# Delta rule: the triangular solve's two steps per half-level on ScalarE instead of VectorE, with N masked by GpSimd and the sums formed in PSUM

## The chip, the cores and the metric

The kernel runs on one core of a Trainium2 chip. The metric is the device time of one execution in microseconds; a comparison uses the median of several runs. Engine names are those of the profile: PE is TensorE (matrix products), PEld its weight loads, DVE is VectorE, ACT is ScalarE, POOL is GpSimd and SP is SyncE, which here only issues DMA. Each engine takes its instructions strictly in the order of its own queue and waits at semaphores for the others.

## The reference

One decoder layer over a prompt of 1024 tokens and 64 sample tokens, in fp32: RMSNorm, one input projection, two parallel token mixers (retention, and RWKV-7 time mixing), output projection, a product-key expert mixer (PEER) and a gated input embedding. The change touches the RWKV-7 scan, which for each of 8 heads with 64 channels is a delta rule:

```python
def step(S, xs):
    rt, lwt, kt, kkt, at, vt = xs
    sa = jnp.einsum('bhij,bhj->bhi', S, -kkt)
    S = (S * jnp.exp(lwt)[:, :, None, :] + sa[..., None] * (kkt * at)[:, :, None, :]
         + vt[..., None] * kt[:, :, None, :])
    y = jnp.einsum('bhij,bhj->bhi', S, rt)
    return S, y
```

## The kernel before, in words

Tokens come in nine tiles: 0 to 7 are 128 prompt tokens each, tile 8 holds the 64 sample tokens. The scan is done per tile in its chunked form. With the masked products of the tile's vectors in Q (L801 to L804), the corrections U of a tile solve a triangular system, U = (I - strict part)^-1 X, for all 8 heads.

*The solve* (L821 to L852). Z starts as the inverse within pairs of tokens: a DVE product with a mask (L824) and an addition of the identity on POOL (L825). N is Q transposed (L818, L819). Five levels m = 2, 4, 8, 16, 32 then double the blocks that are inverted; tile 8 has two. The heads are two halves s of four. At each level and half (a "half-level"):

- PE transposes Z (L837), and ACT copies it to Tt (L839);
- PE multiplies N with the odd blocks' columns Zs of Z, 4 products of 64 columns into pG (L842), and DVE copies that to G, times a 0/1 mask for the level (L844);
- PE multiplies Tt and G into pZG (L849), and DVE adds that to Zs in place (L851).

The three PSUM tiles of a half come from tag "b" with three buffers (tiles 0 and 8: "b" and "d").

*After the solve.* DVE scales the state into S0 (L857). pX is the product of the state with the tile's vectors plus Kq times V, in one PSUM tile (L868 to L876); ACT copies it to X (L879). For prompt tiles the last step of the inverse is done by halves of 64 tokens: U of the lower half (L901, L903), its part in the upper half into pL (L895), added to X by DVE (L897), then U of the upper half. The new state (L908, L918, L919) and the output pY (L963, L964) follow.

*What runs beside it.* `group_b` goes over the tiles in the order 1, 8, 2 to 7 and interleaves three or four generators: the solve and the rest of one tile (`cur`), the retention and preparation of the next up to "chain" (`nxt`), the output projection of an earlier tile (`c_rows`: weights cw streamed from memory, products ewo, L610), and `early`. Each `yield` hands over to the next generator. The framework then sets the order on each engine's queue by its own simulated timeline, so the order moves as a whole when instructions change.

`early` is the expert mixer of tiles 0, 1 and 8. A short query phase loads ewq (L1189) and multiplies (epq, L1194). Then, for each of 128 (tile 8: 64) expert slots, POOL issues an indirect DMA that gathers 128 rows of 4 KB (grow, L1126) into one of four slots of a ring, and DVE uses it: with in_pu in L1140 (a dot product with x, which lies in PSUM), with in_pv in L1154 (added to gacc in PSUM).

After the tiles come the queries of the dense part (`c_query`, PE), the top-k of tiles 4 to 7 (DVE, with what is left of `early`), and a dense pass over all experts (py, ph). Tile 0's solve runs earlier, from 150 to 210 us, beside the input projection.

Of the kernel before, what the change touches and what calls it, by code (L numbers as in the profile page):

```python
# [44 lines left out]
def consts():  # L45
# [26 lines left out]
    lev = np.zeros((128, 5, 64), np.float32)  # L72
    for i, m in enumerate(LEVELS):
        for qq in range(64):
            b = qq // m
            lev[b * 2 * m:b * 2 * m + m, i, qq] = 1.0
# [134 lines left out]
class K:  # L211
# [46 lines left out]
    def setup_mix(self, es):  # L258
# [435 lines left out]
    def rw_mix(self, t):  # L694
# [132 lines left out]
        lev = self.c("lev").rearrange("p (l q) -> p l q", l=5)  # L827
        nq = n // 2
        for li, m in enumerate(LEVELS):
            if smp and m >= 8:  # L830
                break
            Zs = Z[:n, :, :n].rearrange("p h (c s m) -> p h c s m", s=2, m=m)[:, :, :, 1, :]
            Tt, G, pz = [None] * 2, [None] * 2, [None] * 2
            for s in range(2):
                p = self.ps("trz", hb[s]).rearrange("p (a b) -> p a b", a=4)
                for j in range(4):
                    nc.tensor.transpose(p[:n, j, :n], Z[:n, 4 * s + j, :n], self.c("ident", n)[:, :n])  # L837
                Tt[s] = wp.tile([128, 4, n], F32, name=f"Tt{s}")
                nc.scalar.activation(Tt[s][:n, :, :n], p[:n, :, :n], AF.Copy)  # L839
                p = self.ps("pG", hb[s])[:, :256].rearrange("p (h q) -> p h q", h=4)  # L840
                for j in range(4):
                    nc.tensor.matmul(p[:n, j, :nq], N[:n, 4 * s + j, :n], Zs[:, 4 * s + j], start=True, stop=True)  # L842
# [700 lines left out]
```

## Time and profile before

| | us |
|---|---|
| median of 3 runs | 3937.49 |
| the runs | 3921.43, 3937.49, 3937.65 |
| the profiled execution | 3941.76 |
| its span, first to last instruction | 3940.0 |
| PE busy | 3367.7 (85%) |
| DVE busy | 2961.7 (75%) |
| POOL busy | 2339.6 (59%) |
| ACT busy | 1225.5 (31%) |
| mean granted clock of TensorE | 0.87 |

The page comes from one execution. In the rows of groups, the columns are line, engine, operation, tiles (out<-in), shape and count, then busy time in us and mean ns of one, then the engine's idle time just before them and what ended it. An fp32 product appears as two records, a transpose as one. A busy PE is not PE at its peak, since matmuls are pipelined and their ends are modelled.

### The profile page before, as it was taken

The page shows a single profiled execution, that of the slowest core. Times are in us where ns is not written, and L with a number is a line of the kernel's source. Part 1 is how long each engine was busy: PE and PEld are TensorE (multiplying, and loading weights), DVE is VectorE, ACT ScalarE, POOL GpSimd, SP SyncE. Part 2 cuts the span into 40 slices and gives each one's busy share as a digit, 9 for nine tenths or more (in the row PEclk, how much of TensorE's full clock was granted, in tenths as well). Part 3 has the DMA queues.
Part 4 walks back from the last instruction along what each step waited for, and adds up shares of the span by engine and source line. Part 5 has one row for each costly group of instructions (what it writes and reads, how often), then busy time and mean ns, then how long its engine had stood idle before and what let it go on. Part 6 is the DMA issues. An engine that isn't in the chain of part 4 may idle for free.

```text
span 3940.0 us, 52682 instructions
## 1 busy us (share of the span) xinstructions
PE 3367.7 (85%) x17749; PEld 2768.7 (70%) x17749; DVE 2961.7 (75%) x5764; ACT 1225.5 (31%) x2247; POOL 2339.6 (59%) x2051
## 2 busy tenths in 40 slices
PE   8798985777869776885899899999699988999978
PEld 7687984645747664763788678888588866677757
DVE  4454488977697689886659999987777777777774
ACT  4232221011111111111232266777422333333322
POOL 5353175544454536554567757886488777777740
PEclk9799995666977567676999999999899999999989
DMA  7267568898868878789998748899899999999962
GB/s 256 72 194 234 168 209 266 277 302 267 295 229 285 299 269 283 265 278 332 331 350 295 245 171 302 306 347 344 324 343 341 334 362 357 358 362 349 339 230 70
DMA packets 473864, 1107.20 MB, mean 281 GB/s; under 512 B 74555, under 2 KB 191545, under 8 KB 467642
## 3 DMA queue, kind: packets, MB, share of 16 engines
q0 software_dynamic: 165888, 604.05, 43.0%
q1 hardware_dynamic: 245694, 393.26, 30.5%
q10 hardware_dynamic: 62012, 106.52, 7.2%
q8 instruction: 141, 2.31, 0.2%
q14 instruction: 129, 1.06, 0.1%
HBM read 997.17 MB, written 106.43 MB: 280 GB/s over the span
## 4 chain that ended last, share of the span: by engine, by line
PE 45%; DVE 22%; DMA 16%; issue 7%; POOL 6%; ACT 2%; SPq 0%; ACTq 0%; POOLq 0%; DVEq 0%
PE py L1294 14%; DVE grow L1140 4%; DVE gacc L1154 3%; PE ph L325 3%; PE ph L326 3%; PE ph L327 3%; POOL grow L1126 3%; DMA ewq<-in_wq 2%; PE epq L1194 2%; DMA grow<-in_pv,eid 2%; DMA grow<-in_pu,eid 2%; POOL vl L300 2%; DMA ft<-fd 1%; DVE oh L1240 1%; PE ewo L610 1%
## 5 line engine op out<-in xcount | busy, mean ns | idle before, releaser
L1126 POOL DMA_INDIRECT grow<-in_pv,eid x576 | 569.8, 989 | 507.3 <-DVE gacc L1154 309.4
L1126 POOL DMA_INDIRECT grow<-in_pu,eid x576 | 568.7, 987 | 435.2 <-DVE grow L1140 287.9
L1154 DVE SCALAR_TENSOR_TENSOR gacc<-grow,ac,gacc 128x1024 f32<-128x1024 f32 x571 | 731.8, 1282 | 89.5 <-DMA grow<-in_pv,eid 84.3
L1140 DVE SCALAR_TENSOR_TENSOR grow<-grow,gacc 128x1024 f32<-128x1024 f32 x576 | 691.1, 1213 | 125.0 <-DMA grow<-in_pu,eid 118.3
L1294 PE MATMUL py<-ah,vh 128*128 128x512 f32 x1024 | 408.1, 399 | 40.3 <-ACT ah L296 27.1
L1294 PE MATMUL py<-ah,vl 128*128 128x512 f32 x1024 | 407.1, 403 | 34.1 <-POOL vl L300 34.0
L325 PE MATMUL ph<-cx,uh 128*128 128x512 f32 x1024 | 406.4, 397 | 7.2 <-ACT geh L1262 7.2
L326 PE MATMUL ph<-cx,uh 128*128 128x512 f32 x1024 | 406.4, 397 | 0.0
L327 PE MATMUL ph<-cx,ul 128*128 128x512 f32 x1024 | 405.5, 396 | 1.0 <-POOL ul L300 1.0
L1294 PE MATMUL py<-al,vh 128*128 128x512 f32 x1024 | 405.3, 396 | 0.0
L300 POOL TENSOR_TENSOR vl<-vraw,vh 128x640 fp32r<-128x640 f32 (+2 forms) x224 | 325.4, 1457 | 53.1 <-ACT vh L296 49.3
L300 POOL TENSOR_TENSOR ul<-uraw,uh 128x1024 fp32r<-128x1024 f32 x128 | 308.6, 2412 | 64.5 <-ACT uh L296 62.3
L296 ACT ACTIVATE vh<-vraw 128x640 fp32r<-128x640 f32 (+2 forms) x224 | 154.9, 692 | 393.8 <-PE py L1294 238.3
L1294 PEld LDWEIGHTS py<-ah,vl 128*128 128x128 f32 x1024 | 194.1, 190 | 98.4 <-POOL vl L300 56.1
L1294 PEld LDWEIGHTS py<-ah,vh 128*128 128x128 f32 x1024 | 194.6, 190 | 96.5 <-ACT vh L296 28.7
L1298 DVE TENSOR_TENSOR yT<-yT,py 128x512 f32<-128x512 f32 x216 | 147.4, 684 | 151.5 <-PE py L1294 151.1
L325 PEld LDWEIGHTS ph<-cx,uh 128*128 128x128 f32 x1024 | 194.7, 190 | 48.4 <-ACT geh L1262 8.8
L1294 PEld LDWEIGHTS py<-al,vh 128*128 128x128 f32 x1024 | 194.0, 189 | 43.7
L327 PEld LDWEIGHTS ph<-cx,ul 128*128 128x128 f32 x1024 | 194.9, 190 | 41.6 <-POOL ul L300 1.9
L326 PEld LDWEIGHTS ph<-cx,uh 128*128 128x128 f32 x1024 | 195.0, 190 | 39.1
L296 ACT ACTIVATE uh<-uraw 128x1024 fp32r<-128x1024 f32 x128 | 135.2, 1056 | 246.1 <-PE ph L326 128.5
L300 POOL TENSOR_TENSOR wl<-wraw,wh 128x1024 fp32r<-128x1024 f32 x45 | 110.5, 2455 | 138.8 <-ACT wh L296 138.7
(400 smaller groups left out, 7833.3 us busy)
## 6 DMA issues: line engine op xcount, KB each, us to landing
uraw<-in_puT SPq DMA_DIRECT2D x128, 512.0 KB, 4.8
vraw<-in_pvd SPq DMA_DIRECT2D x152, 320.0 KB, 6.1
cw<-in_w_out SPq DMA_DIRECT2D x128, 256.0 KB, 5.1
wd<-wst ACTq DMA_DIRECT2D x32, 1024.0 KB, 13.1
wt<-wd SPq DMA_DIRECT2D x64, 512.0 KB, 8.0
wraw<-in_w_ret SPq DMA_DIRECT2D x48, 512.0 KB, 4.7
ewq<-in_wq SPq DMA_DIRECT2D x48, 512.0 KB, 6.7
gd<-geh ACTq DMA_DIRECT2D x96, 256.0 KB, 5.0
```

The costliest lines, as they stand in the source:

```text
L296: nc.scalar.activation(hi, src, AF.Copy)
L300: nc.gpsimd.tensor_tensor(lo, src, hi.bitcast(F32), op=OP.subtract)
L325: mm(out, lh(k), rh(k), start=first and k == 0, stop=False)
L326: mm(out, lh(k), rl(k), start=False, stop=False)
L327: mm(out, ll(k), rh(k), start=False, stop=last and k == nk - 1)
L610: nc.tensor.matmul(p[:n], oT[k // 4][:, k % 4, :n], w, start=k == 0, stop=k == 7)
L1126: nc.gpsimd.indirect_dma_start(out=g, out_offset=None, in_=src, in_offset=bass.IndirectOffsetOnAxis(ap=self.eid[t][:, j:j + 1], axis=0))
L1140: nc.vector.scalar_tensor_tensor(g[:, c], g[:, c], 1.0, x[:, c], op0=OP.mult, op1=OP.mult, accum_out=hv[:, i, j:j + 1])
L1154: nc.vector.scalar_tensor_tensor(y[:, c], g[:, c], ac[:, j:j + 1], y[:, c], op0=OP.mult, op1=OP.add)
L1194: nc.tensor.matmul(p[:, :n], w[:, k], xT[:, k, :n], start=k == 0, stop=k == 7)
L1294: nc.tensor.matmul(p, lh[:, b, :], rh, start=b == 0 and j == 0, stop=b == nb - 1 and j == 2)
L1298: nc.vector.tensor_tensor(yT[:, d, :], yT[:, d, :], p, op=OP.add)
```

## The change

GpSimd masks N ahead of the solve: `mask(i)` writes Nm, the N of half-level i times that level's 0/1 mask, now 128 columns wide per level. Two masks are issued before the first half-level, and the one for i + 2 within half-level i; Nm has three buffers. pG is then the product of Nm with Zs and needs no mask, so ACT copies it to G. The sum Z + pZG is formed in PSUM: a product of the identity with Zs (256 columns) opens the accumulation, the four products of Tt and G add to it, and ACT copies the result back to Zs. No DVE instruction is left in the half-level. In a level, pG and the transpose of each half come first (the product now ahead of the transpose), then both pZG.

For prompt tiles, pX is made in two PSUM tiles, one for each half of the tokens ("d" and "b"), each with its own state and V products; the former pL accumulates on the upper one, and ACT copies each half to X. The scaled state S0 is made ahead of the levels. To make room, N has one buffer instead of two, S0 one instead of two, and sg moves into the six-buffer tag t2. Tile 8 keeps its pX.

```diff
-               ("lev", 64 * 5), ("hind", 32), ("seqtok", 8), ("seqfeat", 512), ("gc", 4), ("gc8", 8)):
+               ("lev", 128 * 5), ("hind", 32), ("seqtok", 8), ("seqfeat", 512), ("gc", 4), ("gc8", 8)):
...
-        self.Sb = [[cp.tile([128, 4, 128], F32, name=f"S{a}{b}") for b in range(2)] for a in range(3)]
+        self.Sb = [[cp.tile([128, 4, 128], F32, name=f"S{a}{b}") for b in range(1 + (a < 2))] for a in range(3)]
...
-        sg = wp.tile([128, 512], F32, name="sg")
+        sg = T2("sg") if n == 128 else wp.tile([128, 512], F32, name="sg", tag="t2", bufs=6)
...
-        N = wp.tile([128, 8, n], F32, name="N", bufs=b2)
+        N = wp.tile([128, 8, n], F32, name="N")
...
-            for s in range(2):
-                p = self.ps("trz", hb[s]).rearrange("p (a b) -> p a b", a=4)
-                for j in range(4):
-                    nc.tensor.transpose(p[:n, j, :n], Z[:n, 4 * s + j, :n], self.c("ident", n)[:, :n])
-                Tt[s] = wp.tile([128, 4, n], F32, name=f"Tt{s}")
-                nc.scalar.activation(Tt[s][:n, :, :n], p[:n, :, :n], AF.Copy)
-                p = self.ps("pG", hb[s])[:, :256].rearrange("p (h q) -> p h q", h=4)
-                for j in range(4):
-                    nc.tensor.matmul(p[:n, j, :nq], N[:n, 4 * s + j, :n], Zs[:, 4 * s + j], start=True, stop=True)
-                G[s] = wp.tile([128, 4, n // 2], F32, name=f"G{s}")
-                nc.vector.tensor_tensor(G[s][:n, :, :nq], p[:n, :, :nq], lev[:n, li, None, :nq].to_broadcast([n, 4, nq]), op=OP.mult)
-                yield
-            for s in range(2):
-                p = self.ps("pZG", hb[s])[:, :256].rearrange("p (h q) -> p h q", h=4)
-                for j in range(4):
-                    nc.tensor.matmul(p[:n, j, :nq], Tt[s][:n, j, :n], G[s][:n, j, :nq], start=True, stop=True)
-                pz = p[:n, :, :nq].rearrange("p h (c m) -> p h c m", m=m)
-                nc.vector.tensor_tensor(Zs[:, 4 * s:4 * s + 4], Zs[:, 4 * s:4 * s + 4], pz, op=OP.add)
-                yield
...
+        def mask(i):
+            if i < len(steps):
+                li, s = steps[i]
+                Nm[i] = wp.tile([128, 4, n], F32, name="Nm", bufs=3)
+                nc.gpsimd.tensor_tensor(Nm[i][:n, :, :n], N[:n, 4 * s:4 * s + 4, :n],
+                                        lev[:n, li, None, :n].to_broadcast([n, 4, n]), op=OP.mult)
+
+        mask(0)
+        mask(1)
+        for i, (li, s) in enumerate(steps):
...
+            for j in range(4):
+                nc.tensor.matmul(p[:n, j, :nq], Nm[i][:n, j, :n], Zs[:, 4 * s + j], start=True, stop=True)
+            G[s] = wp.tile([128, 4, n // 2], F32, name=f"G{s}")
+            nc.scalar.activation(G[s][:n, :, :nq], p[:n, :, :nq], AF.Copy)
+            mask(i + 2)
+            p = self.ps("trz", hb[s]).rearrange("p (a b) -> p a b", a=4)
...
+            for s in range(2):
+                p = self.ps("pZG", hb[s])[:, :256].rearrange("p (h q) -> p h q", h=4)
+                zs = Zs[:, 4 * s:4 * s + 4]
+                pz = p[:n, :, :nq].rearrange("p h (c m) -> p h c m", m=m)
+                nc.tensor.matmul(pz, self.c("ident", n)[:, :n], zs, start=True, stop=False)
+                for j in range(4):
+                    nc.tensor.matmul(p[:n, j, :nq], Tt[s][:n, j, :n], G[s][:n, j, :nq], start=False, stop=j == 3)
+                nc.scalar.activation(zs, pz, AF.Copy)
+                yield
...
+            px = {}
+            for half, tag in ((lo, "d"), (up, "b")):
+                p = px[tag] = self.ps("pX", tag)
+                opens = True
+                for hp in range(4):
+                    if not first:
+                        nc.tensor.matmul(p[half, hp * 128:hp * 128 + 128], art[:, hp, 0, half], S0[:, hp, :], start=opens, stop=False)
+                        opens = False
+                    for s in range(2):
+                        h = 2 * hp + s
+                        hs = slice(h * 64, h * 64 + 64)
+                        nc.tensor.matmul(p[half, hs], Kq[:, hq(h), 0, half], V[:, hs], start=opens, stop=half is lo and h == 7)
+                        opens = False
+                yield
...
-                        nc.tensor.matmul(p[up, hs], Q[lo, hq(h), 0, up], U[lo, hs], start=True, stop=True)
+                        nc.tensor.matmul(p[up, hs], Q[lo, hq(h), 0, up], U[lo, hs], start=False, stop=h == 7)
                     yield
-                    nc.vector.tensor_tensor(X[up], X[up], p[up], op=OP.add)
+                nc.scalar.activation(X[half], p[half], AF.Copy)
```

How the order moves is seen in the last tile's solve. DVE's queue there before (gacc<-grow are the gathered rows being used, G and Z the solve):

```order
L981 TENSOR_TENSOR hnx<-hnx,pgt 128x512
L844 TENSOR_TENSOR G_12617<-pG,cstb 128x256
L1154 SCALAR_TENSOR_TENSOR gacc<-grow,ac,gacc 128x1024
L844 TENSOR_TENSOR G_12631<-pG,cstb 128x256
L1154 SCALAR_TENSOR_TENSOR gacc<-grow,ac,gacc 128x1024
L851 TENSOR_TENSOR Z<-Z,pZG 128x128x2 x2
L1154 SCALAR_TENSOR_TENSOR gacc<-grow,ac,gacc 128x1024
L844 TENSOR_TENSOR G_12671<-pG,cstb 128x256
```

and DVE's queue there after the change, up to the tile's new state (S<-pS):

```order
L1007 TENSOR_TENSOR hnx<-hnx,pgt 128x512
L1180 SCALAR_TENSOR_TENSOR gacc<-grow,ac,gacc 128x1024 x10
L610 TENSOR_TENSOR ch<-ewo,ch 128x512
L1180 SCALAR_TENSOR_TENSOR gacc<-grow,ac,gacc 128x1024 x4
L944 TENSOR_TENSOR S_204<-pS,S_205 64x4x64 x2
```

The solve's 20 instructions are gone from between the gathered rows. POOL's queue in the same solve before (grow<-in_pv are the gathers being issued, Z and hnx the tile's own work):

```order
L825 TENSOR_TENSOR Z<-Z,csta 128x1024
L1126 DMA grow<-in_pv,eid_65 128x1024
L970 TENSOR_TENSOR hnx<-hnx,row_ln_g 128x512
L1126 DMA grow<-in_pv,eid_65 128x1024
L971 TENSOR_TENSOR hnx<-hnx,row_ln_b 128x512
L1126 DMA grow<-in_pv,eid_65 128x1024 x2
L974 TENSOR_TENSOR hnx<-hnx,bv 128x512
L1126 DMA grow<-in_pv,eid_65 128x1024 x24
```

and POOL's queue after the change (Nm are the masks):

```order
L838 TENSOR_TENSOR Nm<-N,cstb 128x512
L1152 DMA grow<-in_pv,eid_65 128x1024
L838 TENSOR_TENSOR Nm<-N,cstb 128x512
L1152 DMA grow<-in_pv,eid_65 128x1024
L1000 TENSOR_TENSOR hnx<-hnx,bv 128x512
L838 TENSOR_TENSOR Nm<-N,cstb 128x512
L1152 DMA grow<-in_pv,eid_65 128x1024
L838 TENSOR_TENSOR Nm<-N,cstb 128x512
L1152 DMA grow<-in_pv,eid_65 128x1024 x2
L838 TENSOR_TENSOR Nm<-N,cstb 128x512
```

A run of 24 gathers has become gathers and masks in turn.

More of the change, by code (lines that the diff above doesn't have):

```diff
@@ L71, in consts @@
     put("rel8", rel8)
[L72 to L76, printed above, removed]
+    same = lambda m: p[:, None] // (2 * m) == p[None] // (2 * m)
+    lev = np.stack([same(m) & (p[:, None] // m % 2 == 1) & (p[None] // m % 2 == 0) for m in LEVELS], 1).astype(np.float32)
     put("lev", lev)
@@ L826, in rw_mix @@
         yield "chain"
[L827 to L833, printed above, removed]
[L834 to L852 removed]
         if not first and not smp:
[L854 removed]
+            S0 = self.Sb[2][0]
             for s in range(2):
@@ L857, in rw_mix @@
                 nc.vector.tensor_tensor(S0[ps_, :, ps_], self.Swkv[ps_, :, ps_], pe[ps_, 0, :, None].to_broadcast([64, 4, 64]), op=OP.mult)
+        lev = self.c("lev").rearrange("p (l q) -> p l q", l=5)
+        nq = n // 2
+        steps = [(li, s) for li, m in enumerate(LEVELS) if not smp or m < 8 for s in range(2)]
+        Nm = {}
+        def mask(i):
[7 more added lines that the diff above has]
+        for i, (li, s) in enumerate(steps):
+            m = LEVELS[li]
+            if s == 0:
+                Zs = Z[:n, :, :n].rearrange("p h (c s m) -> p h c s m", s=2, m=m)[:, :, :, 1, :]
+                Tt, G = [None] * 2, [None] * 2
+            p = self.ps("pG", hb[s])[:, :256].rearrange("p (h q) -> p h q", h=4)
+            for j in range(4):
[5 more added lines that the diff above has]
+            for j in range(4):
+                nc.tensor.transpose(p[:n, j, :n], Z[:n, 4 * s + j, :n], self.c("ident", n)[:, :n])
+            Tt[s] = wp.tile([128, 4, n], F32, name=f"Tt{s}")
+            nc.scalar.activation(Tt[s][:n, :, :n], p[:n, :, :n], AF.Copy)
+            yield
+            if s == 0:
+                continue
+            for s in range(2):
[3 more added lines that the diff above has]
+                nc.tensor.matmul(pz, self.c("ident", n)[:, :n], zs, start=True, stop=False)
+                for j in range(4):
+                    nc.tensor.matmul(p[:n, j, :nq], Tt[s][:n, j, :n], G[s][:n, j, :nq], start=False, stop=j == 3)
+                nc.scalar.activation(zs, pz, AF.Copy)
+                yield
         def state_mm(p, hp, j):
@@ L867, in rw_mix @@
         hq = lambda h: (h % 2) * 4 + h // 2
[L868 to L877 removed]
         X = T3("X")
[L879 removed]
         U = T3("U")
         if smp:
+            p = self.ps("pX", "d")
+            for hp in range(4):
+                sq = state_mm(p, hp, 0)
+                for s in range(2):
+                    h = 2 * hp + s
+                    hs = slice(h * 64, h * 64 + 64)
+                    self.seq_mm(p[:n, hs], *sq, s)
+                    nc.tensor.matmul(p[:n, hs], Kq[:n, hq(h), 0, :n], V[:n, hs], start=False, stop=True)
+            yield
+            nc.scalar.activation(X[:n], p[:n], AF.Copy)
             p = self.ps("pU", "d")
```

23 lines of the change are left out of this document (8 added, 15 removed).

## The prediction

> **What bounds the kernel now.** I read the stages first, then the groups of instructions within the stage that holds the change, then who waits there, then the chain. The page gives the span; the windows give the stages (columns: stretch, its length, busy time of PE, PEld, DVE, ACT and POOL with counts, granted clock, DMA share, GB/s).
>
> ```profile
> span 3940.0 us, 52682 instructions
> ...
> 150.00:200.00 50.00, 49.26 (x351) 44.60 (x351) 21.87 (x46) 13.63 (x22) 7.36 (x8) 0.88 0.09 30
> ...
> 600.00:1000.00 400.00, 291.58 (x1516) 210.29 (x1516) 318.84 (x533) 46.64 (x105) 202.60 (x198) 0.63 0.87 279
> 1000.00:1400.00 400.00, 317.57 (x1669) 261.27 (x1669) 299.24 (x620) 58.16 (x138) 199.88 (x198) 0.69 0.81 276
> 1400.00:1810.00 410.00, 327.37 (x1761) 255.96 (x1760) 351.25 (x684) 64.45 (x125) 220.91 (x220) 0.74 0.82 280
> 1900.00:2000.00 100.00, 99.16 (x610) 88.36 (x609) 64.95 (x103) 28.32 (x50) 57.38 (x51) 1.00 0.92 342
> ...
> 2100.00:2200.00 100.00, 96.14 (x420) 78.29 (x420) 100.00 (x429) 28.02 (x35) 77.11 (x54) 1.00 0.81 277
> ...
> 2400.00:2500.00 100.00, 95.39 (x487) 80.03 (x486) 99.97 (x214) 65.94 (x130) 82.81 (x62) 0.98 0.91 330
> ```
>
> Tile 0's solve lies in 150 to 200 us, where PE is full (49.26 of 50). The other eight solves lie between 600 and 1810 us. There no engine is full: DVE 969 us of 1210, PE 936, POOL 623, ACT 169. Queries follow (PE full), then the top-k stage, where DVE is full. So I ask what paces 600 to 1820 us. The groups in it:
>
> ```profile
> L1154 DVE SCALAR_TENSOR_TENSOR gacc<-grow,ac,gacc 128x1024 f32<-128x1024 f32 x229 | 293.3, 1281 | 50.9 <-DMA grow<-in_pv,eid 49.3
> L1140 DVE SCALAR_TENSOR_TENSOR grow<-grow,gacc 128x1024 f32<-128x1024 f32 x233 | 280.4, 1212 | 61.0 <-DMA grow<-in_pu,eid 59.4
> L1126 POOL DMA_INDIRECT grow<-in_pv,eid x234 | 238.2, 1018 | 301.3 <-DVE gacc L1154 216.4 <-DMA grow<-in_pv,eid 24.5 <-DVE hns L409 11.4
> L1126 POOL DMA_INDIRECT grow<-in_pu,eid x230 | 227.1, 987 | 250.9 <-DVE grow L1140 193.8 <-issue 13.5 <-DVE G L844 7.2
> ...
> L610 PE MATMUL ewo<-cw,coT 128*128 128x512 f32 (+1 forms) x224 | 124.2, 666 | 14.4 <-DMA cw<-in_w_out 10.6 <-issue 2.1 <-DVE S L506 0.7
> ...
> L842 PE MATMUL pG<-Z,N 128*128 128x64 f32 (+1 forms) x592 | 93.5, 313 | 0.0
> ...
> L844 DVE TENSOR_TENSOR G<-pG,cstb 128x256 f32<-128x256 f32 (+1 forms) x74 | 30.3, 410 | 31.4 <-PE pG L842 31.1
> L851 DVE TENSOR_TENSOR Z<-Z,pZG 128x256 f32<-128x256 f32 (+1 forms) x74 | 29.6, 405 | 11.2 <-PE pZG L849 10.6
> ...
> L825 POOL TENSOR_TENSOR Z<-Z,csta 128x1024 f32<-128x1024 f32 (+1 forms) x8 | 17.8, 2220 | 1.0 <-DVE Z L824 0.9
> ```
>
> The gathers are a ring: POOL issues a row gather into one of four slots, it lands, DVE uses it, and only then may POOL refill the slot. 234 + 230 gathers in 1220 us are one per 2.63 us, 10.5 us per turn of a slot. The issue rows (last number: us to landing) and the waits (total us, times, longest) show what the turn is made of.
>
> ```profile
> grow<-in_pv,eid POOLq DMA_INDIRECT x234, 6.4
> grow<-in_pu,eid POOLq DMA_INDIRECT x230, 5.8
> ```
> ```profile
> POOL grow L1126 <- DVE gacc L1154: 216.4, 137, 7.1
> POOL grow L1126 <- DVE grow L1140: 200.8, 151, 11.1
> ```
> ```profile
> DVE grow L1140 <- DMA grow<-in_pu,eid: 59.4, 53, 3.3
> DVE gacc L1154 <- DMA grow<-in_pv,eid: 49.3, 38, 4.2
> DVE G L844 <- PE pG L842: 31.1, 22, 3.9
> ...
> DVE Z L851 <- PE pZG L849: 10.6, 13, 1.4
> ```
>
> A bare turn is 5.8 to 6.4 us to landing plus 1.21 to 1.28 us on DVE, 7.0 to 7.7. The other 2.8 to 3.5 us are time in which the row lies landed and DVE is at something else: DVE waited for a landing only 53 + 38 times in 462, while POOL waited for DVE to release a slot 137 + 151 times in 464. So the ring paces this stage, and DVE's queue is its loose part. The solve's own instructions on DVE (L844, L851) are part of that, with what DVE idles in front of them. The chain says the same (share of 600 to 1820 us):
>
> ```profile
> by line: issue 8.5%; DMA ewq<-in_wq 7.2%; DVE grow L1140 6.9%; DMA grow<-in_pv,eid 5.9%; PE epq L1194 5.5%; DMA grow<-in_pu,eid 4.7%; DVE gacc L1154 4.7%; DMA ft<-fd 4.4%; POOL grow L1126 3.8%; PE ewo L610 3.1%; PE pZG L849 2.5%; PE pG L842
> ```
>
> Gathers hold 26% of it (6.9 + 5.9 + 4.7 + 4.7 + 3.8). The early query's serial weight loads (ewq, epq) hold 12.7%, and the change touches nothing there. The solve appears with PE products at 2.5% or less; its DVE lines are not among the first twelve.
>
> **The change part by part.** The profiled execution took 3941.76 us, 4 above the median of the runs (3937.49). The sum is made against 3941.76 and then moved to the median. Between 600 and 1820 us there are 74 half-levels (7 tiles of 10, tile 8 with 4).
>
> *Off DVE.* 74 x (0.410 + 0.405) us = 60 us of work and 31.4 + 11.2 = 43 us of idling before it leave DVE's queue, and per tile one L897 of 0.69 us:
>
> ```profile
> L897 DVE TENSOR_TENSOR X<-X,pL x8: 691/691/692, 218.9 to 1789.0; 64x512 f32<-64x512 f32 x8
> ```
>
> That is 5 us for seven tiles, 108 us together. A delay on DVE holds one slot; the other three are under way. So I take a quarter: **-27 us**. Bounds: all 108 if DVE bounds the stage by itself, 0 if the gathers fill the holes with waiting for landings.
>
> *Onto ACT.* The copies of G and Z are 128x256 out of PSUM. That form is in the trace, as is ACT's wait for the solve's transposes:
>
> ```profile
> L395 ACT ACTIVATE retd<-pret x18: 366/384/387, 48.4 to 454.3; 128x256 f32<-128x256 f32 x16, 64x256 f32<-64x256 f32 x2
> ```
> ```profile
> ACT Tt L839 <- PE trz L837: 243.4, 63, 35.9
> ```
>
> 0.38 us on ACT against 0.41 on DVE, 57 us in all on an engine busy for 169 of 1210. In 63 of 74 cases ACT stood waiting for PE, so it is free when a product comes: 0. If that cover went (ACT stuck on something else in its queue), each of the 148 copies would be late by that.
>
> *Onto POOL.* One mask per half-level, 128x512 with two inputs. L825 is the same kind at twice the width, 2.22 us on average, its narrow tile-8 form included; half is 1.1, and I take 1.2. 74 x 1.2 = 89 us, in a queue that idles 301.3 + 250.9 = 552 us before 464 gathers, 1.19 us each. A mask just about fills one such hole; with a semaphore hop it hangs over. I take 0.5 us each, 37 us, on one slot of four: **+9 us**. Bounds: 0 (masks are issued two half-levels ahead) and 89 (every mask in full in front of a gather whose slot is free).
>
> *New wait on POOL.* The first mask of a tile waits for ACT's copy of N, and later masks for a buffer that PE has read. Behind it in POOL's queue stand the gathers, and DVE's products behind those. The nearest row is DVE's own wait for the first product, which also needs N: up to 3.9 us, 31.1 in all. The gathers give way in one slot of four: **+4 us** for 7 tiles, bounds 0 and 31.
>
> *Onto PE.* The identity product is 256 columns; L610 takes 124.2 us for 112 products of 512 columns (two records each), so 0.55 us for 256, 41 us in all. pX in halves adds 12 products a tile. L842 has 93.5 us for 296 products of 64 columns, 0.32 us each, so 27 us more. PE is idle for 274 of the 1210 us and is not in the ring: 0 there, bounds 0 and 68. In tile 0's solve PE is full, so there its ten identity products count, and a few halves: **+6 us**.
>
> *Order.* Counted over the whole of DVE's order, 473 gathered rows are used before the last tile's state is written, and 464 after the change; before the first candidates of the later top-k 275 rows of in_pv against 258. So the solve stage carries 9 gathers fewer, 9 x 2.63 = 24 us, and the top-k stage, with DVE full, 17 more at 1.28 us, 22 us. That cancels: 0, bounds -24 and +22. The ring's mended buffers (one N, one scaled state, sg in t2) wait for things that stand earlier in program order anyway: 0.
>
> *The shared port.* Once in the trace a POOL add and a DVE product from two SBUF inputs meet:
>
> ```profile
> 1732.46 2.33 POOL L825 TENSOR_TENSOR Z<-Z,csta 128x1024 f32<-128x1024 f32 x1
> ...
> 1732.98 2.37 DVE L417 TENSOR_TENSOR hnx<-hnx,hnr 128x512 f32<-128x512 f32 x1
> ```
> ```profile
> L417 DVE TENSOR_TENSOR hnx<-hnx,hnr x18: 671/682/2365, 111.9 to 1817.2; 128x512 f32<-128x512 f32 x16, 64x512 f32<-64x512 f32 x2
> ```
>
> The meeting costs DVE 1.69 us over the median. From these rows alone I charge nothing, since the gathers' own DVE lines keep 1.2 to 1.3 us on average beside a POOL that is busy half the time. The Trainium skill, "SBUF — State Buffer", on the shared port pair, says that GpSimd and a VectorE instruction with two SBUF inputs exclude each other for the whole of an instruction. That speaks against this change: 89 us of masks are 7% of the stage. If some 120 DVE instructions there have such inputs (my count from the code), some 8 would meet a mask and lose about 0.6 us, 5 us: by the rule the sum would be up to 5 us higher.
>
> **Sum:** -27 + 9 + 4 + 6 + 0 = -8 us: 3934 against 3941.76, and **3930 us** against the median 3937.49.
>
> **The rivals.** A measurement of this kernel can tell about 0.5%, 20 us, from no change.
>
> *Faster: DVE bounds the stage by itself.* For it: from 1400 to 1810 DVE is busy 351 of 410 us, and POOL waits for DVE more than for anything. Then DVE's removed work counts in full, 60 + 5 us, and the rest stays: -65 + 9 + 6 = -50, some 3888 us. Against it: a bare turn still needs 7 us per slot, and the early query's loads and products hold 12.7% of the chain, 155 us, in which DVE is not waited for. Chance 0.36 for faster by over 20 us.
>
> *Slower: POOL takes DVE's place in the ring.* In POOL's order the last tile's ten masks alternate with ten gathers. A gather (0.99 us) and a mask (1.2) with their hops of some 0.2 us are 2.6 us, as long as the ring's step of 2.63. From the point where a mask is issued later than the slot in front of which it stands comes free, all of it delays the ring, for all four slots, since POOL issues in order. With half the masks so, 44 us, and the gain on DVE gone in waiting for landings: +44 + 6 = +50, some 3988 us. Against it: the masks run two half-levels ahead. Chance 0.23 for slower by over 20 us.
>
> *The change does not do what it says.* The order rules this out: between the last tile's Z and its state no DVE row of the solve is left.
>
> **How the numbers follow.** The forecast case, within 20 us of the median, has 0.41, the faster one 0.36, the slower one 0.23. The forecast's own range is 3918 to 3957. The range for 8 in 10 reaches to the faster case (3888, and 8 us further for its idling) and most of the slower one: 3880 to 3978.
>
> **What would show it.** Right, if the profile after has no DVE wait for PE in the solve, gathers between 600 us and the last state stepping by 2.5 to 2.6 us, POOL's idling before gathers down by some 60 us, and the solve's copies on ACT at 0.38 us. Wrong towards faster, if that step falls under 2.5 us; wrong towards slower, if waits of POOL's masks for ACT or PE, or DVE's waits for landings (109 us now), grow by more than 40 us, or if PE's solve products take a visibly larger share of the chain.

## The result and the profile after

| | before | after |
|---|---|---|
| median of the runs, us | 3937.57 (4 runs, 3921.43 to 3940.35) | 3990.47 (4 runs, 3979.17 to 3996.58) |
| the profiled execution, us | 3941.76 | 3979.17 |

The change is slower: 1.014 times the time before, 95% interval 1.0104 to 1.0175, 53 us between the medians. The prediction, 3930 with a range of 3880 to 3978, was wrong. The two profiled executions lie 37 us apart; what is read from traces is set against that.

The page and the windows after (columns as before):

```profile
span 3977.2 us, 53641 instructions
...
600.00:1000.00 400.00, 269.83 (x1446) 194.76 (x1447) 310.15 (x498) 57.33 (x137) 215.31 (x211) 0.67 0.86 278
1000.00:1400.00 400.00, 314.88 (x1862) 254.17 (x1861) 294.41 (x557) 78.24 (x191) 227.51 (x221) 0.74 0.80 267
1400.00:1810.00 410.00, 330.77 (x1953) 257.19 (x1952) 324.41 (x614) 92.17 (x199) 251.91 (x248) 0.80 0.80 271
```

DVE did get lighter (929 us of 1210, 969 before), POOL heavier (695, 623 before). The groups from 600 to 1820 us:

```profile
L1166 DVE SCALAR_TENSOR_TENSOR grow<-grow,gacc 128x1024 f32<-128x1024 f32 x234 | 281.0, 1214 | 82.5 <-DMA grow<-in_pu,eid 76.2 <-ACT gacc L1160 5.0
L1180 DVE SCALAR_TENSOR_TENSOR gacc<-grow,ac,gacc 128x1024 f32<-128x1024 f32 x214 | 274.5, 1283 | 82.5 <-DMA grow<-in_pv,eid 80.6
L1152 POOL DMA_INDIRECT grow<-in_pu,eid x231 | 231.1, 1000 | 207.5 <-DVE grow L1166 153.6 <-issue 14.0 <-ACT gacc L1160 7.9
L1152 POOL DMA_INDIRECT grow<-in_pv,eid x219 | 223.4, 1020 | 242.9 <-DVE gacc L1180 169.5 <-DMA grow<-in_pv,eid 19.6 <-issue 11.6
...
L838 POOL TENSOR_TENSOR Nm<-N,cstb 128x512 f32<-128x512 f32 (+1 forms) x74 | 79.8, 1086 | 38.0 <-PE pG L850 25.0 <-ACT N L689 12.3
...
L866 PE MATMUL pZG<-Z,csta 128*128 128x256 f32 (+1 forms) x148 | 49.3, 419 | 4.4 <-ACT G L852 3.1 <-ACT Tt L858 1.3
...
L869 ACT ACTIVATE Z<-pZG 128x256 f32<-128x256 f32 (+1 forms) x74 | 28.2, 382 | 94.5 <-PE pZG L868 86.9 <-DVE hnx L1007 4.0 <-issue 3.6
L852 ACT ACTIVATE G<-pG 128x256 f32<-128x256 f32 (+1 forms) x74 | 28.0, 378 | 82.1 <-PE pG L850 78.3 <-DVE hnx L1007 3.6
```

448 rows are used where 462 were. The solve is gone from DVE, but what DVE waits for has changed. The waits of the ring in the same stretch:

```profile
POOL grow L1152 <- DVE gacc L1180: 169.5, 111, 9.4
POOL grow L1152 <- DVE grow L1166: 158.8, 132, 7.7
...
DVE gacc L1180 <- DMA grow<-in_pv,eid: 80.6, 56, 3.8
...
DVE grow L1166 <- DMA grow<-in_pu,eid: 76.2, 65, 4.0
...
POOL Nm L838 <- PE pG L850: 25.0, 18, 4.1
...
POOL Nm L838 <- ACT N L689: 12.3, 5, 4.7
```

DVE waits 157 us for landings (109 before), POOL 328 us for DVE (417 before): the slack in the ring has moved from POOL's side to DVE's. This is the sign that the prediction named for "wrong towards slower" (landing waits up by more than 40 us). POOL's idling before gathers fell by 102 us (450, 552 before), more than the 60 that the prediction named as a sign of being right; but 118 us of masks and of waits in front of them had come into POOL's queue.

Where the 37 us come up is read from first use to last state, and from the top-k to the first product of the dense part. The uses on DVE from 545 us to the last state, before (to 1796 us) and after (to 1802 us):

```profile
L1140 DVE SCALAR_TENSOR_TENSOR grow<-grow,gacc 128x1024 f32<-128x1024 f32 x256 | 308.0, 1212 | 69.3 <-DMA grow<-in_pu,eid 67.8
L1154 DVE SCALAR_TENSOR_TENSOR gacc<-grow,ac,gacc 128x1024 f32<-128x1024 f32 x218 | 279.2, 1281 | 47.0 <-DMA grow<-in_pv,eid 45.4
```
```profile
L1166 DVE SCALAR_TENSOR_TENSOR grow<-grow,gacc 128x1024 f32<-128x1024 f32 x256 | 307.5, 1214 | 91.3 <-DMA grow<-in_pu,eid 85.0 <-ACT gacc L1160 5.0
L1180 DVE SCALAR_TENSOR_TENSOR gacc<-grow,ac,gacc 128x1024 f32<-128x1024 f32 x208 | 266.8, 1283 | 79.9 <-DMA grow<-in_pv,eid 78.0
```

474 uses in 1251 us are a step of 2.64 us, 464 in 1257 are 2.71. Ten rows fewer should have ended the stage 26 us earlier; the longer step took 32, so it ends 6 us later. The later top-k and the dense products, before and after (first and last start):

```profile
L1042 DVE MAX8 sv<-s x96: 265/274/295, 2069.9 to 2367.0; 128x8 f32<-128x128 f32 x96
...
L1294 PE MATMUL py<-ah,vh x1024: 387/389/794, 2819.2 to 3767.9; 128*128 128x512 f32 x171
```
```profile
L1068 DVE MAX8 sv<-s x96: 264/275/296, 2071.9 to 2365.2; 128x8 f32<-128x128 f32 x96
...
L1320 PE MATMUL py<-ah,vh x1024: 387/389/792, 2857.2 to 3805.0; 128*128 128x512 f32 x171
```

The top-k starts 2 us later, the dense part 38. Between them DVE uses 16 rows more:

```profile
2070.00:2819.00 749.00, 672.95 (x3344) 563.94 (x3342) 680.26 (x1925) 444.11 (x858) 517.07 (x373) 0.96 0.80 289
...
L1140 DVE SCALAR_TENSOR_TENSOR grow<-grow,gacc 128x1024 f32<-128x1024 f32 x128 | 153.0, 1210 | 11.1 <-DMA grow<-in_pu,eid 11.1
L1154 DVE SCALAR_TENSOR_TENSOR gacc<-grow,ac,gacc 128x1024 f32<-128x1024 f32 x55 | 70.0, 1273 | 6.6 <-DMA grow<-in_pv,eid 6.4
```
```profile
2072.00:2857.00 785.00, 679.75 (x3334) 572.88 (x3332) 694.61 (x1942) 441.58 (x857) 531.18 (x389) 0.93 0.79 284
...
L1166 DVE SCALAR_TENSOR_TENSOR grow<-grow,gacc 128x1024 f32<-128x1024 f32 x128 | 152.2, 1212 | 23.5 <-DMA grow<-in_pu,eid 23.4
L1180 DVE SCALAR_TENSOR_TENSOR gacc<-grow,ac,gacc 128x1024 f32<-128x1024 f32 x71 | 90.7, 1277 | 10.9 <-DMA grow<-in_pv,eid 10.5
```

The stretch is 36 us longer, 14 of them DVE's work and 22 its idling. If all of it is put down to the 16 rows, each row that is not used beside the solve comes back as 2.25 us, not 1.28. Order alone does much of this: in e5 below, where no instruction changes, 16 rows more stand there too, and the stretch is 25 us longer.

### The profile page after: what moved, and what is told of

Read it like the earlier page. It is cut to its first block, busy times and chain, and to the rows that moved or that the text cites. A ratio compares the mean times of both kernels' runs of the same rounds, so it can differ in the third digit from the quotient of the medians.

```text
span 3977.2 us, 53641 instructions
## 1 busy us (share of the span) xinstructions
PE 3353.3 (84%) x18101; PEld 2759.4 (69%) x18101; DVE 2923.1 (73%) x5588; ACT 1289.7 (32%) x2423; POOL 2428.3 (61%) x2134
## 4 chain that ended last, share of the span: by engine, by line
PE 42%; DVE 23%; DMA 17%; issue 8%; POOL 7%; ACT 2%; SPq 0%; ACTq 0%; POOLq 0%; DVEq 0%
PE py L1320 13%; DVE grow L1166 4%; DMA grow<-in_pu,eid 3%; POOL grow L1152 3%; DVE gacc L1180 3%; DMA grow<-in_pv,eid 3%; PE ph L322 2%; PE ph L324 2%; PE ph L323 2%; DMA vraw<-in_pvd 2%; DMA ewq<-in_wq 2%; PE epq L1220 2%; POOL vl L297 2%; PE pwt L1271 2%; DVE oh L1266 1%
## 5 line engine op out<-in xcount | busy, mean ns | idle before, releaser
L1180 DVE SCALAR_TENSOR_TENSOR gacc<-grow,ac,gacc 128x1024 f32<-128x1024 f32 x571 | 732.5, 1283 | 120.6 <-DMA grow<-in_pv,eid 114.6
L1166 DVE SCALAR_TENSOR_TENSOR grow<-grow,gacc 128x1024 f32<-128x1024 f32 x576 | 689.8, 1214 | 160.6 <-DMA grow<-in_pu,eid 145.5
L1271 PE MATMUL pwt<-oh,oh 128*128 128x128 f32 x1024 | 161.3, 309 | 61.8 <-ACT oh L1268 61.1
```

The source lines that it names most:

```text
L1166: nc.vector.scalar_tensor_tensor(g[:, c], g[:, c], 1.0, x[:, c], op0=OP.mult, op1=OP.mult, accum_out=hv[:, i, j:j + 1])
L1180: nc.vector.scalar_tensor_tensor(y[:, c], g[:, c], ac[:, j:j + 1], y[:, c], op0=OP.mult, op1=OP.add)
L1271: nc.tensor.matmul(pw[:, j, :], oh[1][:, j, :], oh[0][:, j, :], start=True, stop=True)
```

## The experiments

Three theories stood at first. **M**: POOL's masks hold up the gathers. **O**: the framework's new order puts fewer rows ahead of the late stages. **P**: the added products on PE. All ratios are against the kernel before on the same chip, with 95% intervals; further readings of every run are in the table at the end of this section.

*e1, masks undone.* G is masked again by DVE, N is used as it is, the old 64-column mask is back; the rest of the change stays.

```diff
-                nc.tensor.matmul(p[:n, j, :nq], Nm[i][:n, j, :n], Zs[:, 4 * s + j], start=True, stop=True)
+                nc.tensor.matmul(p[:n, j, :nq], N[:n, 4 * s + j, :n], Zs[:, 4 * s + j], start=True, stop=True)
...
-            nc.scalar.activation(G[s][:n, :, :nq], p[:n, :, :nq], AF.Copy)
-            mask(i + 2)
+            nc.vector.tensor_tensor(G[s][:n, :, :nq], p[:n, :, :nq], lev[:n, li, None, :nq].to_broadcast([n, 4, nq]), op=OP.mult)
```

> The changed kernel without POOL's masks: N is used as it is, and DVE masks G as it copies it from PSUM, as before the change; the rest stays (Z's sum in PSUM with ACT's copy, pX by halves, the order of a level). The changed kernel took 3990, the kernel before 3937, 53 us apart. Theory M (masks: in POOL's own order the 80 us of masks and the 37 us that POOL waits in front of them hold up the gathers): without them the gathers between 600 us and the last state step by about 2.6 us again, DVE's waits for landings fall back from 157 to about 110 us, and the time is 3925 to 3945. Theory O (order: the order has 485 gathered rows used ahead of the second expert query's weights' first use on DVE, where the kernel before has 501; each row put off costs about 3.3 us later): here it is 488, so 3970 to 3985. Theory P (PE: the identity products and pX by halves, 106 us of PE work in the stage): they are all still there, so about 3990.

Measured 3961.9 against 3931.3: 1.0081 [1.0054, 1.0108]. Less than half of the loss goes. The time lies between M's range and O's, and 28 us below P's; DVE's landing waits fall from 157 to 135 us, not to 110.

*e2, masks twice.*

```diff
                 nc.gpsimd.tensor_tensor(Nm[i][:n, :, :n], N[:n, 4 * s:4 * s + 4, :n],
                                         lev[:n, li, None, :n].to_broadcast([n, 4, n]), op=OP.mult)
+                nc.gpsimd.tensor_tensor(Nm[i][:n, :, :n], N[:n, 4 * s:4 * s + 4, :n],
+                                        lev[:n, li, None, :n].to_broadcast([n, 4, n]), op=OP.mult)
```

> The changed kernel with each of POOL's masks issued twice in a row (the second writes the same values again). M: another 80 us of work in POOL's queue, so another half to the whole of the loss: 4015 to 4045, and DVE's waits for landings rise from 157 to 200 us or more. O: the order here has 508 gathered rows ahead of that landmark, 23 more than the changed kernel and 7 more than the kernel before, so 3915 to 3940. P: about 3990.

Measured 4018.2: 1.0207 [1.0166, 1.0248]. The order with the most rows ahead so far gave the longest time, so O as written falls; M's range for the time holds. The masks in this run from 600 to 1820 us, first and second of each pair:

```profile
L838 POOL TENSOR_TENSOR Nm<-N,cstb 128x512 f32<-128x512 f32 (+1 forms) x69 | 74.6, 1088 | 63.5 <-PE pG L852 47.6 <-ACT N L689 15.2 <-issue 0.3
L840 POOL TENSOR_TENSOR Nm<-N,cstb 128x512 f32<-128x512 f32 (+1 forms) x68 | 73.0, 1076 | 1.1
```

The second set is 73 us more of POOL's work, and 0.67% of the time (26 us) came with it. DVE's landing waits did not go to 200 us, as M expected, but to 167; DVE also uses 11 rows fewer there.

*e3, old pX; e4, old sum of Z.* e3 puts back the old lines of pX, pL and X, e4 those of Z's sum:

```diff
-            for half, tag in ((lo, "d"), (up, "b")):
-                p = px[tag] = self.ps("pX", tag)
...
+        p = self.ps("pX", "d")
...
+                    p = self.ps("pL", "d")
...
+                    nc.vector.tensor_tensor(X[up], X[up], p[up], op=OP.add)
```
```diff
-                nc.tensor.matmul(pz, self.c("ident", n)[:, :n], zs, start=True, stop=False)
...
-                nc.scalar.activation(zs, pz, AF.Copy)
+                nc.vector.tensor_tensor(zs, zs, pz, op=OP.add)
```

> The changed kernel with the old pX: one PSUM tile, a copy to X, pL apart and its sum on DVE (and so 28 us less on PE and 5 us more on DVE). Masks and identity products stay. M: 3980 to 3995. O: 506 gathered rows ahead of the landmark, so 3920 to 3940. P: 28 of 106 us of added PE work are gone, a quarter of the 53: 3970 to 3980.

> The changed kernel with the old sum of Z: no identity product, DVE adds pZG to Zs in place. Masks and pX by halves stay; 30 us of work and some 11 us of waiting come back to DVE and 49 us of products leave PE. M: masks stay and DVE gets work back, 3990 to 4010. O: 505 gathered rows ahead of the landmark, 3920 to 3940. P: half of the added PE work gone, 3960 to 3970.

Measured 3972.6, 1.0120 [1.006, 1.018], and 3981.0, 1.0126 [1.0085, 1.0167]. Neither mends it. O's ranges are missed by 33 and 41 us; M's are missed by 7 and 9 on the low side. e3 lies in P's range, but e4, which takes out the identity products, lies 11 us above it.

*e5 to e7, order moved.* Only the offset of the early gathers' priority changes: -100 in the kernel before, 60 in the changed one, 30 in e1's kernel.

```diff
-PE_ = 0
+PE_ = -100
```

> The kernel before with every instruction kept; only the offset of the early gathers' priority goes from 0 to -100, and the order then stands as after the change: 464 gathered rows used ahead of the last state and 590 ahead of the later top-k (before: 473 and 604; after: 464 and 588). Theory M+ (POOL's masks slow the ring from 2.63 to 2.70 us per gather; of the order only the rows count that fall out of the queries, where PE sets the pace, into the top-k, where each costs DVE some 2.2 us): 9 rows fewer at 2.63 us bring the last state 24 us earlier, 14 rows more in the top-k cost 31, so 3931 + 7, some 3938. Theory O+ (the 31 us by which the run without masks stayed above the kernel before are the order): that run had 468 and 590, so 3955 to 3965 here. Theory R (they are the rest of the change: identity products, pX by halves, products ahead of transposes, the single buffers): none of that is here, so 3925 to 3937.

> The changed kernel with every instruction kept; the offset of the early gathers' priority goes from 0 to 60, and the order then stands as before the change: 472 gathered rows ahead of the last state, 603 ahead of the later top-k. M+: the masks stay, so 2.69 to 2.70 us per gather, 472 x 0.065 = 31 us: 3960 to 3970. O+: 31 of the 53 us go, 3950 to 3958. R: nothing goes, 3980 to 3995.

> The changed kernel without POOL's masks (DVE masks G as it copies it) as in the first run, and the offset of the early gathers' priority at 30: 477 gathered rows ahead of the last state, 605 ahead of the later top-k. M+: 2.63 us per gather as before the change; 4 rows more cost 10, one row fewer later gains 2: 3935 to 3945. O+: the order is mended and the masks are gone, and DVE has 46 us less of the solve: 3920 to 3932. R: identity products, pX by halves and the level's order stay: 3955 to 3968.

Measured: e5 3953.9, 1.0037 [1.0021, 1.0054]; e6 4000.2, 1.0170 [1.0148, 1.0193]; e7 3956.7, 1.0057 [1.0033, 1.0081]. e5 lies above M+ and R and just short of O+, e6 above every range, e7 in R's. Rows ahead of two landmarks do not give the time. But e5 shows, with no instruction changed, that order alone costs.

*e8 to e12, one part alone.* e8 is e1's kernel with the old lines of Z's sum (e4) and of pX (e3) besides, so the old solve in the new level with the single buffers; e9 the level's new order and the earlier scaled state alone; e10 the single buffers alone; e11 the sum of Z alone; e12 that and pX by halves. The edits of e9, e10 and e11:

```diff
-                p = self.ps("trz", hb[s]).rearrange("p (a b) -> p a b", a=4)
...
             p = self.ps("pG", hb[s])[:, :256].rearrange("p (h q) -> p h q", h=4)
...
+            p = self.ps("trz", hb[s]).rearrange("p (a b) -> p a b", a=4)
```
```diff
-        N = wp.tile([128, 8, n], F32, name="N", bufs=b2)
+        N = wp.tile([128, 8, n], F32, name="N")
...
-            S0 = self.Sb[2][t % 2]
+            S0 = self.Sb[2][0]
...
-        sg = wp.tile([128, 512], F32, name="sg")
+        sg = T2("sg") if n == 128 else wp.tile([128, 512], F32, name="sg", tag="t2", bufs=6)
```
```diff
+                nc.tensor.matmul(pz, self.c("ident", n)[:, :n], zs, start=True, stop=False)
...
-                nc.vector.tensor_tensor(Zs[:, 4 * s:4 * s + 4], Zs[:, 4 * s:4 * s + 4], pz, op=OP.add)
+                nc.scalar.activation(zs, pz, AF.Copy)
```

> The solve and pX as before the change (G masked and Z added on DVE, one pX, pL apart), but the level's new order (product pG ahead of the transpose), the scaled state ahead of the levels, N and the scaled state in one buffer each and sg in t2. The order has 465 gathered rows ahead of the last state and 590 ahead of the later top-k, as the kernel before with its order moved. M+: 465 rows at 2.63 us, 21 us earlier, and 14 rows later, 31: about 3940. O+: 3955 to 3965. R, if it is the level's order or the single buffers: 3955 to 3968; if it is PE's added products: 3925 to 3940.

> The kernel before with one edit: in a level, pG and the transpose of each half stand as after the change (the product ahead of the transpose) and the scaled state is made ahead of the levels. Solve on DVE, one pX, two buffers of N and of the scaled state, sg of its own. 464 gathered rows stand ahead of the last state and 592 ahead of the later top-k, as in the kernel before when only its order was moved (464 and 590, which measured 1.0037 of before). The run with the old solve in the new level and the single buffers measured 1.011 [1.007, 1.015]. Theory L (the level's order causes what that has above the order alone): 1.009 to 1.013, 3967 to 3983. Theory B (the single buffers of N and the scaled state and sg in t2 cause it): 1.002 to 1.006, 3940 to 3956. Theory S (neither: the pace of the ring scatters by some 0.05 us per gather from order to order): anything from 1.002 to 1.013, and the pace alone tells it.

> The kernel before with only the change's buffers: one N and one scaled state instead of two, sg in the six-buffer tag t2. All instructions and the level's order stay. 476 gathered rows stand ahead of the last state, 597 ahead of the later top-k (before: 473 and 604). B: 1.006 to 1.010, 3956 to 3972. L: 1.000 to 1.004, 3933 to 3948, since 3 rows more ahead of the state and 7 more in the top-k are some 20 us of which a part falls together. S: 1.000 to 1.011.

> The kernel before with only the sum of Z moved: the identity product opens pZG and ACT copies the sum to Zs. G is still masked by DVE as it is copied; no masks on POOL, pX, buffers and the level's order as before. DVE loses 30 us of work and 11 us of waiting, PE gets about 45 us. 482 gathered rows stand ahead of the last state, 611 ahead of the later top-k (before: 473 and 604). If DVE's removed work speeds the ring up by a quarter of itself, as the prediction had it (10 of 41 us): 3915 to 3930. If it does nothing for the ring: 3930 to 3945. S: 3935 to 3970.

> The kernel before with the sum of Z in PSUM and on ACT and with pX by halves (no pL, no sum on DVE): all of the change but the masks on POOL, the level's order and the buffers. 476 gathered rows stand ahead of the last state, 605 ahead of the later top-k, as near to the order before (473, 604) as the run of the changed kernel without masks and with its order moved (477 and 605, 1.0057 of before), which has the new level and the single buffers besides. L or B: 0.996 to 1.001, 3916 to 3937. S: 1.000 to 1.010. If the identity products and pX by halves themselves cost: 1.004 to 1.008, like that run.

Measured: e8 3982.6, 1.0110 [1.0068, 1.0153]; e9 3966.4, 1.0086 [1.0054, 1.0119]; e10 3976.4, 1.0108 [1.0074, 1.0141]; e11 3951.0, 1.0037 [1.0017, 1.0057]; e12 3969.8, 1.0088 [1.0056, 1.0120]. e8 is above every range. e9 lies just under L's range and e10 just over B's, and both can't be the one cause. e11 is 21 us above the range that the prediction's quarter gave. e9 to e12 all lie in S's. Parts that have nothing in common each cost 0.4 to 1.1%. That speaks for theory S: the kernel before stands in an unusually good order, and an edit draws a new one.

*e13 to e18, the same offset in both kernels.* The offset is 100, 300 and 30, in the kernel before and in the changed one, as in the diff of e5.

> The kernel before, all instructions kept, offset of the early gathers' priority 100 instead of 0: 479 gathered rows ahead of the last state, 607 ahead of the later top-k (473 and 604 at offset 0). Theory S (the order that stood before is a lucky one of many, any other costs 0.4 to 1.1%): 1.003 to 1.011 of before. Theory X (an order with about as many rows ahead costs nothing, and the 0.4 to 1.1% of the runs with one part each are these parts' own): 0.997 to 1.003.

> The kernel before, all instructions kept, offset 300: 481 gathered rows ahead of the last state, 610 ahead of the later top-k. S: 1.003 to 1.011 of before. X: 0.997 to 1.003.

> The changed kernel, all instructions kept, offset 100: 477 gathered rows ahead of the last state, 609 ahead of the later top-k. If one set of masks costs 25 us (the mean of the runs with masks over the mean of those without, 1.0139 against 1.0075) whatever the order: 1.011 to 1.018 of before, pace 2.66 to 2.72 us per gather. If the loss was this one order's: 1.003 to 1.010.

> The changed kernel, all instructions kept, offset 300: 484 gathered rows ahead of the last state, 620 ahead of the later top-k, the most of any run. Masks cost whatever the order: 1.011 to 1.018, pace 2.66 to 2.72. The loss was the order's: 1.003 to 1.010, or less if rows ahead of the top-k are what counts.

> The kernel before, all instructions kept, offset 30: 465 gathered rows ahead of the last state, 593 ahead of the later top-k. The four orders of it so far lie at 1.000, 1.004, 1.013 and 1.020. S (its own order is a lucky one): 1.003 to 1.020. If it is not: 0.995 to 1.003.

> The changed kernel, all instructions kept, offset 30: 463 gathered rows ahead of the last state, 589 ahead of the later top-k, nearly the counts of the kernel before at the same offset. If the change itself costs some 25 to 30 us whatever the order (the means of four orders each are 1.009 and 1.018): 0.004 to 0.012 above the kernel before at this offset, a pace some 0.05 us longer, and DVE's waits for landings 40 to 60 us longer. If the change itself costs nothing: within 0.003 of it.

| offset | before, ratio | after, ratio | apart |
|---|---|---|---|
| 0 | 1 | 1.0140 [1.0104, 1.0175] | 1.4% |
| 30 (e17, e18) | 1.0078 [1.0046, 1.0110] | 1.0195 [1.0143, 1.0247] | 1.2% |
| 100 (e13, e15) | 1.0127 [1.0092, 1.0163] | 1.0193 [1.0128, 1.0259] | 0.7% |
| 300 (e14, e16) | 1.0197 [1.0159, 1.0234] | 1.0229 [1.0194, 1.0264] | 0.3% |
| -100 (e5), 60 (e6) | 1.0037 [1.0021, 1.0054] | 1.0170 [1.0148, 1.0193] | |

Outside their ranges, all upward, are e13 and e14 (S), e15 and e16 (masks); e17 and e18 are inside, with DVE's landing waits 72 us apart where 40 to 60 were expected. X falls: the kernel before, with all its instructions, is up to 2% slower in other orders, and its own is the best of five. The changed kernel is slower at each common offset, by 0.9% or 35 us in the mean of the four pairs, from 13 to 55 us; at 100 and 300 the two intervals overlap. The means over five orders each are 1.0088 and 1.0185: 38 us apart.

What stays the same from order to order is in the table, all from 600 to 1820 us: the gathered rows used on DVE; how many times POOL stood waiting for DVE to release a slot; DVE's waits for landings in us; and by how many us DVE's instructions were drawn out (the sum, in the trace, of each one's time over the median of its line and tiles, where over 0.1 us).

| run | ratio | uses | POOL waits for DVE, times | landing waits, us | drawn out, us |
|---|---|---|---|---|---|
| before, five orders | 1 to 1.020 | 446 to 466 | 270 to 298 | 91 to 112 | 19 to 26 |
| after, five orders | 1.014 to 1.023 | 437 to 452 | 191 to 243 | 154 to 169 | 40 to 48 |
| e3, e4 (masks stay) | 1.012, 1.013 | 456, 448 | 218, 215 | 174, 117 | 43, 36 |
| e2 (masks twice) | 1.021 | 437 | 189 | 167 | 35 |
| e1, e7 (no masks, Z on ACT) | 1.008, 1.006 | 459, 459 | 281, 290 | 135, 132 | 25, 28 |
| e8 to e12 (one part or two) | 1.004 to 1.011 | 445 to 469 | 261 to 287 | 92 to 113 | 20 to 31 |

One column sorts all runs by their masks: the eight kernels with masks have 189 to 243 such waits of POOL, the twelve without 261 to 298. With masks, more slots are already free when POOL comes to them. Landing waits do not sort them so. They are high where masks and Z's sum on ACT come together (154 to 174 us); Z's sum on ACT without masks has 92 to 135 (e1, e7, e11, e12), and masks with Z's sum on DVE have 117 (e4). These are e4's rows:

```profile
POOL grow L1151 <- DVE gacc L1179: 172.7, 103, 10.0
POOL grow L1151 <- DVE grow L1165: 154.4, 112, 9.4
```
```profile
DVE grow L1165 <- DMA grow<-in_pu,eid: 63.3, 57, 3.9
DVE gacc L1179 <- DMA grow<-in_pv,eid: 53.5, 45, 5.5
```

The times agree with the masks. The eight kernels with them lie at 1.012 to 1.023, 1.0173 in the mean, the twelve without at 1 to 1.020, 1.0084 in the mean; only e13 and e14 of the twelve are over 1.011. That is 0.9% or 35 us apart.

The matched pair at offset 30, whose orders have nearly the same rows ahead, shows it in rows. Before (e17), then after (e18), from 600 to 1820 us:

```profile
POOL grow L1126 <- DVE gacc L1154: 212.3, 134, 6.2
POOL grow L1126 <- DVE grow L1140: 200.1, 136, 8.5
...
DVE grow L1140 <- DMA grow<-in_pu,eid: 50.5, 47, 3.1
...
DVE gacc L1154 <- DMA grow<-in_pv,eid: 43.5, 35, 3.8
```
```profile
POOL grow L1152 <- DVE grow L1166: 157.2, 110, 11.1
POOL grow L1152 <- DVE gacc L1180: 153.2, 81, 12.2
...
DVE grow L1166 <- DMA grow<-in_pu,eid: 94.5, 64, 8.2
...
DVE gacc L1180 <- DMA grow<-in_pv,eid: 71.4, 51, 3.7
...
POOL Nm L838 <- PE pG L850: 37.5, 15, 6.5
...
POOL Nm L838 <- ACT N L689: 16.5, 8, 6.6
```

None of the eighteen beats the kernel before; e11, the nearest, has an interval that ends at 1.0017.

## Why the prediction was wrong

*Off DVE, -27 us: this step failed.* The work left DVE, but the ring did not step faster: in the mean of five orders each, DVE used 457 rows in the stretch before and 447 after. What DVE gained it spent waiting for landings, 102 us on average before and 160 after. The prediction saw POOL waiting for DVE 288 times and took DVE for the loose part. By the same rows POOL did not wait for a use on DVE in the other 176 of 464 gathers, and after the change in 207 of 450. A POOL that waits less for DVE only matters if its next gather then goes out, and masks stood there. Without masks too, POOL's waits for DVE did not shrink when DVE lost Z's sum: 408 to 441 us in e1, e7, e11 and e12, 399 to 463 in the five orders before. e11's trace does use more rows than any other, 469, but it is of the fastest of ten executions (3929 us, median 3951).

*Onto POOL, +9 us: mis-sized.* One mask took 1.09 us (1.2 said), but a quarter of a 0.5 us overhang was too little. The masks' price was three times read from pairs of runs: e1 to the changed kernel 0.59% (23 us), e7 to e6 1.13% (44), the changed kernel to e2 0.67% (26). Each pair also differs in order, and the changed kernel's own orders lie up to 0.9% apart, so no pair is proof by itself. They agree in sign and size with the 35 us between all kernels with masks and all without, and e1, e7 and e8, which keep the level's order and the single buffers without masks, lie below every kernel with masks.

*New wait on POOL, +4 us: mis-sized.* It was priced from DVE's waits for the first product. POOL itself waited 25.0 us for a mask buffer that PE had to read first and 12.3 us for N, 37 in all, and 32 to 54 in the other orders; bound 31. What it cost is part of the masks' price above. The three terms of the ring so far, -14 in the sum, came out at some +33 (the 38 us between the means over five orders, less 5 for tile 0's solve below). How that divides is not fixed: the three pairs give the masks 31 in the mean, which leaves about 0 for the freed DVE; the means of the orders against that of e1 and e7 give 46 and a gain of 13.

*The shared port, 0: wrong.* The prediction took its rows for the one meeting in the trace. In the same stage before, 25 DVE instructions were drawn out beside POOL's computing, by 25 us together. After, DVE's drawn-out time is 43 us on average over five orders, 23 before, with no overlap; some 20 us of it lies beside masks in the changed kernel (14 instructions). Two of them in one stretch, POOL's queue first and DVE's second (start, length):

```profile
1184.16 3.18 POOL L838 TENSOR_TENSOR Nm<-N,cstb 128x512 f32<-128x512 f32 x3
1187.50 1.55 POOL L1152 DMA_INDIRECT grow<-in_pv,eid  x1 [0.16 <-issue]
1189.07 1.76 POOL L1108 TENSOR_TENSOR eq<-eq,ce 128x800 f32<-128x800 f32 x1
1190.77 1.10 POOL L838 TENSOR_TENSOR Nm<-N,cstb 128x512 f32<-128x512 f32 x1
```
```profile
1184.93 3.27 DVE L1107 TENSOR_TENSOR eq<-csta,cf 128x800 f32<-128x800 f32 x1
1188.13 0.68 DVE L1007 TENSOR_TENSOR hnx<-hnx,pgt 128x512 f32<-128x512 f32 x1
1188.72 3.23 DVE L719 TENSOR_SCALAR sf<-sf 128x128 f32<-128x128 f32 x1
```

The usual lengths of the two held instructions in this trace (min/median/max ns):

```profile
L1107 DVE TENSOR_TENSOR eq<-csta,cf x72: 965/984/3642, 489.1 to 2643.2; 128x800 f32<-128x800 f32 x64, 64x800 f32<-64x800 f32 x8
```
```profile
L719 DVE TENSOR_SCALAR sf<-sf x9: 219/314/3234, 133.3 to 1635.7; 128x128 f32<-128x128 f32 x8, 128x64 f32<-128x64 f32 x1
```

L1107 ends 0.86 us after the third mask, about its usual time (0.98), as if it had begun when POOL let go; L719, 0.31 us as a rule, ends with the last of two POOL instructions. The Trainium skill, "SBUF — State Buffer", section "SBUF: two separate sides", gives the rule: the engine that holds the pair keeps it for its whole instruction and the other blocks. The trace agrees, and beside masks DVE lost 20 us of its time, where the prediction's estimate by the same rule was 5: it counted 8 meetings of 0.6 us, where there were 14 of 1.4. How much of these 20 us reached the end is not shown, since DVE also waits for landings; it is part of the masks' price above.

*Order, 0 with bounds of -24 and +22: this step failed too.* The prediction counted rows at two landmarks and let them cancel. In this pair of traces they did not: the 26 us of the ten rows went to the longer step, and 16 rows came back at 2.25 us. And counts are not the price of an order: e13 has more rows ahead than the kernel before, as many uses in the stage, and is 1.3% slower. The five orders of the kernel before spread over 78 us, so that its own order is 35 us better than their mean and the change's own 18 better than the mean of its five: 38 + 35 - 18 = 55, the loss that was measured. By this split the order cost 35 - 18 = 17 us, inside the bound, but not by the counts. Against the prediction's sum the ring is 47 us worse and the order 17. The offsets are no random sample of orders, so this split is rough.

*Right.* ACT's copies took 0.382 and 0.378 us, waiting for PE before nearly all (65 and 64 of 74). The identity products took 49 us (41 said), and taking them out again (e4) did not bring the time back. Tile 0's solve, +6: its state came at 228.1 us and now at 233.3, +5:

```profile
L916 DVE TENSOR_TENSOR S<-pS,pe x2: 418/423/428, 228.1 to 228.6; 64x256 f32<-64x256 f32 x2
```
```profile
L942 DVE TENSOR_TENSOR S<-pS,pe x2: 416/422/427, 233.3 to 233.7; 64x256 f32<-64x256 f32 x2
```

*The rivals.* The slower one (POOL takes DVE's place in the ring, 3988) had the mechanism that the runs bear out: the masks stand in front of gathers, POOL comes later to free slots and waits less for DVE, and DVE, freed of the solve, waits more for landings. Its price of 44 us came from half of the masks; the runs put the masks at 23 to 46. That it met 3990 so closely is partly chance, since some of the 53 us are the order's. The faster rival is refuted for this change: DVE had 40 us less to do and the time rose.

*Open.* Why one order of the same instructions is 15 to 78 us slower than another was not settled; neither rows ahead nor uses in the solve stage give it. How much a freed DVE is worth to the ring without masks stays open too: e1, e7, e11 and e12 lie 9 us below the mean of the five orders before, far inside the orders' spread. Whether the level's order or the single buffers (priced at 0) cost anything of their own can't be told: e8 to e10 lie within the spread of the orders.

## What to carry to other kernels

When a ring is fed by one engine and emptied by another, work taken from the one and given to the other is not a gain by its size: look which of the two waits last after the move. Where a framework lays out the order, first measure how far the same instructions spread over a few orders (here 2%), and believe an edit's effect only against that spread, or by signs that hold in every order, as POOL's waits for DVE did here. Such a sign tells which engine comes late, not what that costs: landing waits were low in e4, and it was as slow as e3.

## What the runs showed of the hardware

In these two cases a DVE instruction that met POOL instructions in a row did not get in between them: L1107 was held through three masks, 3.27 us instead of 0.98, and in e18 an L719 took 4.27 us beside a mask, POOL's L1108 and another mask in a row (0.23 is its median there). A TENSOR_SCALAR with one input in SBUF (L719) was held like those with two. The gathers' own uses on DVE (gacc and x lie in PSUM) were not drawn out: 1214 and 1283 ns, 1212 and 1281 before.
